# A two-layer attention trunk on one core: first loads moved to other tiles, two weight units queued earlier, copies and side stages placed anew

## The chip, the cores and the metric

The kernel runs on one core of one Trainium2 chip. The metric is the device time of one execution in microseconds, the median of the runs shown. TensorE is called PE below, VectorE DVE, ScalarE ACT, GpSimd POOL, SyncE SP.

## The reference, cut to what matters

256 frames of width 1024 pass two layers. Layer 0 is differential attention, layer 1 a sparse attention in which an indexer chooses 64 keys for each query; each is followed by a squared-ReLU MLP of width 4096. All is float32.

```python
h = rms_norm(x, norm_mix[i])
# layer 0
q, k, v = split(h @ w_in)                      # 1024 columns each
q, k = rope(rms_norm(q, q_g)) * d**-0.5, rope(rms_norm(k, k_g))
p = softmax(where(mask, q @ k.T, -inf))        # 16 maps, two for each of 8 heads
o = rms_norm((p[0] - lam * p[1]) @ v, subln_g) @ w_out
# layer 1
c_q, k, v, k_idx, w_idx = split(h @ w_in)
q, q_idx = c_q @ w_uq, c_q @ w_uq_idx
score = sum_h w_idx[h] * relu(q_idx[h] @ k_idx.T)
idx = top_k(where(mask, score, -inf), 64)
o = softmax(q @ k[idx].T) @ v[idx] @ w_out     # 16 heads
# after each
x = x + o
x = x + relu(rms_norm(x, norm_mlp[i]) @ w1)**2 @ w2
```

## The kernel before

**Products in three parts.** Every float32 operand of a large product is split in two: `hi` is the operand rounded to a reduced form that the matmul takes, `lo` the rest. `mm3` issues three matmuls, hi by hi, hi by lo, lo by hi. So a block of weights (a "unit" of 128 by 2048, 1 MB) is loaded into a `raw` tile, then ACT (or DVE) writes `hi` and DVE writes `lo`, and only then can PE use it. `unit` does that: it issues the load on SP's queue, then the copies, in `pieces` of columns. There are three `raw` tiles and four pairs of hi and lo tiles, so a load waits until the `lo` of the unit three before it has been written.

**Layer 0.** Four projections (j = 0 to 3), each 48 matmuls of 512 columns, give queries and keys of two heads each. For each, `qk_post` (ACT squares, DVE sums, rsqrt, scaling, rope) and `diff_probs` (transposes, scores, exponentials, the difference, transposes to keys) follow. Then two projections of the values (`v_part`), the weighted sums and their normalisation (`diff_out`), and the output projection. The normalisation of the rows of x (`row_scale`, two ACT squares over x) is not needed by the projection: it scales the results later, through `s2c` and `scon`.

**The start.** The first projection's x (transposed) and weights come as one packed input, `first_in`: for k = 0 to 3 a block of 256 columns of x and 512 of weights, then the four further blocks of x. Four loads bring it, in order: block 0 with the small constants, block 1, both into `vt` tiles; blocks 2 and 3 together into the first `raw` tile; the further x into the second. Then the first unit (`ua`, in two loads) into the third `raw` tile. `pack` (constants, the identity for transposes, the gains) is loaded next, then a unit called `ahead`, then x, twice 512 KB; the partner of `ahead` is made after the first projection's matmuls.

**Order.** The program is written in one order, and a scheduler gives each engine its queue from it by priority and by the times that it expects; on the chip each engine then works its queue strictly in order. `spawn` starts a generator as a side stage: it runs until it yields a number of ticks, and goes on after so many matmuls of `mm3`. A yield of 0 or less lets it go on at once. `PAUSE` holds the ticks by the stage's name, 0 where there is none. `HOME` holds choices: `pieces n` of the n-th such unit (default 2); `hi n` which piece DVE copies in place of ACT (default none); `qn`, `qkT`, `aT`, `craw`, `qi`, `vt` 1 for DVE and 0 for ACT; `on` 1 for four ACT copies, 0 for one DVE product; `copied` 1 if keys are copied out of PSUM before they are scaled, 0 if the scaling itself reads PSUM (default 1 for a0 and k1); `ez` from which half of the rows on DVE scales the exponentials (0: both, 2: none).

**Layer 1.** A compressed projection, the indexer (`index`: scores, then eight rounds of max and match-replace for each half of the rows, on DVE), keys (k0, k1), queries (q0, q1), values, `dsa_probs` for each half of the heads, the weighted sums (`dsa_out`), the output projection. `need` runs a side stage to its end.

Of the kernel before, what the change touches and what calls it, by code (L numbers as in the profile page):

```python
# [9 lines left out]
F32 = mybir.dt.float32  # L10
# [6 lines left out]
D = 1024  # L17
# [8 lines left out]
C_NORM = 0  # L26
# [11 lines left out]
S_GAIN, S_INV, S_POS, S_K, S_X, S_END = 0, 8, 16, 32, 32 + 4 * 768, 32 + 4 * 768 + 4 * 256  # L38
# [3 lines left out]

PAUSE = {"a1 transposes 0": 6, "a1 transposes 1": 13, "a1 scores 1": 26, "a2 transposes 0": 6,
# [4 lines left out]

HOME = {"copied a1": 1, "qn a1 0": 1, "qkT a1 0": 1, "hi 1": 1, "pieces 2": 1, "aT a2 1": 1, "aT a1 1": 1,
# [5 lines left out]


@with_exitstack
def trunk(ctx: ExitStack, tc: tile.TileContext, x_in, first_in, pack_in, wf, out):
    nc = tc.nc
    E = ctx.enter_context
    const = E(tc.tile_pool(name="const", bufs=1))
    wraw = E(tc.tile_pool(name="wraw", bufs=3))
    wsp = E(tc.tile_pool(name="wsp", bufs=4))
    act = E(tc.tile_pool(name="act", bufs=4))
    qkp = E(tc.tile_pool(name="qkp", bufs=4))  # L70
    vp = E(tc.tile_pool(name="vp", bufs=2))
# [6 lines left out]
    def acc():  # L78
        return psum.tile([128, 512], F32, name="acc", bufs=4)

    def wk():
        return psum.tile([128, 512], F32, name="wk", bufs=4)
# [5 lines left out]
    nc.scalar.preload_act_table_set("trig_and_small")  # L88


    first = [vp.tile([128, D], F32, name="vt") for _ in range(2)]
    raws = [wraw.tile([128, 2048], F32, name="raw") for _ in range(2)]
    src = []

    def load_first(dst, c, a, b):
        nc.sync.dma_start(dst[:, c:c + b - a], first_in[:, a:b])
        src.append((dst, c, a, b))

    def start(a, n):
        for dst, c, lo, hi in src:  # L100
            if lo <= a and a + n <= hi:
                return dst[:, c + a - lo:c + a - lo + n]

    load_first(first[0], 0, 0, S_K + 768)
    load_first(first[1], 0, S_K + 768, S_K + 2 * 768)
    load_first(raws[0], 0, S_K + 2 * 768, S_X)
    load_first(raws[1], 0, S_X, S_END)

    ident = pack[:, C_ID:C_ID + 128]
    cmask = const.tile([128, 384], F32, name="cmask")  # L110
# [12 lines left out]
    def pause(stage):  # L123
        return PAUSE.get(stage, 0)

    def opt(name, d=0):
        return HOME.get(name, d)

# [11 lines left out]
    def advance(e, to_end=False):  # L140
        was, inside[0] = inside[0], True
        while e in side and (to_end or e[0] <= 0):
            try:
                e[0] = next(e[1])
            except StopIteration:
                side.remove(e)
        inside[0] = was

    def spawn(gen):
        e = [0, gen]  # L150
        side.append(e)
        advance(e)
        return e

    def need(*es):
        for e in es:
            advance(e, True)
# [9 lines left out]
    split = []  # L167
# [3 lines left out]
    def unit(cols=2048, dmas=1, pieces=1, each=None, att=False, homes=None):  # L171


        raw = wraw.tile([128, 2048], F32, name="raw")
        if homes is None:
            hi = wsp.tile([128, 2048], F32R, name="whi")
            lo = wsp.tile([128, 2048], F32R, name="wlo")
        src = bass.AP(tensor=wf.tensor, offset=wf.offset + off[0], ap=[[cols, 128], [1, cols]])
        off[0] += 128 * cols
        step = cols // dmas  # L180
        for i in range(dmas):
            c = slice(i * step, (i + 1) * step)
            nc.sync.dma_start(raw[:, c], src[:, c])
        if att:
            units[0] += 1
            pieces = opt(f"pieces {units[0]}", 2)
        if homes is not None:
            return halves(raw, homes)
        step = cols // pieces
        for i in range(pieces):  # L190
            c = slice(i * step, (i + 1) * step)
            with tc.issue_after(each(i)) if each is not None else ExitStack():
                split[:] = [copy(att and opt(f"hi {units[0]}") == i + 1, hi[:, c], raw[:, c]).ins]
            nc.vector.tensor_tensor(lo[:, c], raw[:, c], hi[:, c].bitcast(F32), op=OP.subtract)  # L194
        return hi[:, :cols], lo[:, :cols]

    def halves(raw, homes):

        res = []
        for c, n, tiles in homes:  # L200
            c = slice(c, c + n)
            hi, lo = [a[:, :n] for a in tiles()]
            nc.scalar.activation(hi, raw[:, c], AF.Copy)
            nc.vector.tensor_tensor(lo, raw[:, c], hi.bitcast(F32), op=OP.subtract)
            res.append((hi, lo))
        return res
# [83 lines left out]
    behind = []  # L290
    ready = []
# [227 lines left out]
    def out_proj(o, us, h, gc, needs=((),) * 4):  # L519


        ps = [[acc() for _ in range(2)] for _ in range(2)]
        for u, (wh, wl) in enumerate(us):
            need(*needs[u])
            wh = wh.rearrange("p (k n) -> p k n", n=D)
            wl = wl.rearrange("p (k n) -> p k n", n=D)
            for n in range(2):
                for t in range(2):
                    c = slice(n * 512, n * 512 + 512)
                    for i in range(2):  # L530
                        k = u * 2 + i
                        ah, al = lhs(o, k, t)
                        mm3(ps[t][n], ah, al, wh[:, i, c], wl[:, i, c], k == 0, k == 7)
                    if u == 3:
                        for j in range(2):
                            c = slice(n * 512 + j * 256, n * 512 + j * 256 + 256)
                            nc.vector.tensor_tensor(x[t][:, c], ps[t][n][:, j * 256:j * 256 + 256], x[t][:, c],
                                                    op=OP.add)
                            make_h(h, gc, t, n, (j,))
# [74 lines left out]
    h = new_h()  # L614
# [13 lines left out]
    for k in range(4):  # L628
        first_h(k)
        v, c = start(S_K + 768 * k + 256, 512), slice(512 * k, 512 * k + 512)  # L630
# [6 lines left out]
        return behind[0]  # L637

    ua.append(unit(dmas=2, pieces=4, each=later_h))
    nc.sync.dma_start(pack, pack_in)  # L640
    ahead = unit(pieces=2)
    for t in range(2):
        nc.sync.dma_start(x[t], x_in[t * 128:(t + 1) * 128, :])
    srow, s2 = row_scale(1)
# [35 lines left out]
    o = new_h()  # L680
# [61 lines left out]
    def take():  # L742
        return ready.pop(0) if ready else pair()

    pr = [[] for _ in range(4)]
    probs, outs = [], []
    for j in range(4):
        ps = [acc() for _ in range(2)]
        project(ps, h, quad(take() if j else ua), 512, by_k=j == 0)
        if j == 0:  # L750
            ready.append([ahead, unit(pieces=2)])
            rope_sines(*angles)
            lam()
        probs.append(spawn(diff_probs(ps, pr[j], f"a{j}")))
# [5 lines left out]
    h = new_h()  # L760
# [16 lines left out]
    h = h1  # L777
# [8 lines left out]
    cqh, cql, _ = parts()  # L786
# [96 lines left out]
    craw = compress()  # L883
# [14 lines left out]
    for n in range(2):  # L898
        ps = [acc() for _ in range(2)]
        c = slice(n * 512, n * 512 + 512)  # L900
# [6 lines left out]
    o = new_h()  # L907
# [19 lines left out]
                    out.append(to_keys(e, f"{half} {hd + r}"))  # L927

    def dsa_out(g, aTs):
        ops = wk()  # L930
        for p in range(2):
            c = p * 256
            for r in range(2):
                rows = slice(64 * r, 64 * r + 64)
                a = aTs[2 * p + r]
                vc = (4 * g + 2 * p + r) * 64
                mm(ops[rows, c:c + 256], vts[1][0][:, vc:vc + 64], a[:, 0:256], start=True, stop=False)
                mm(ops[rows, c + 128:c + 256], vts[1][1][:, vc:vc + 64], a[:, 256:384], start=False, stop=True)
        k = 2 * g
        oh = o[k // 4][0][:, k % 4:k % 4 + 2].rearrange("p a b -> p (a b)")  # L940
        ol = o[k // 4][1][:, k % 4:k % 4 + 2].rearrange("p a b -> p (a b)")
        nc.scalar.activation(oh, ops, AF.Copy)
        nc.vector.tensor_tensor(ol, ops, oh.bitcast(F32), op=OP.subtract)  # L943

    for half in range(2):
        aTs = []
        probs = spawn(dsa_probs(half, aTs))
        v_part(half, h, srow)
        need(probs)
        for i in range(2):  # L950
            dsa_out(2 * half + i, aTs[4 * i:4 * i + 4])
    h = new_h()
    out_proj(o, take() + take(), h, C_NORM + 24)

    def store(t, n, j):
        if (t, n) != (1, 1) and j == 0:
# [124 lines left out]
```

## Time and profile before

| | us |
|---|---|
| median of 3 runs (596.99 to 597.17) | 597.13 |
| the profiled execution | 597.93 |
| its span, first to last instruction | 595.7 |
| PE busy, DVE busy, ACT busy (of the span) | 585.3, 433.3, 348.0 |

Some 2.2 us of the profiled execution lie outside of the span. PE is busy 98% of it. A matmul of 512 columns is shown with 0.39 us, but the next one starts 0.23 us later, so up to 0.16 us of a wait is not shown as idle.

### The profile page before, as it was taken

What the parts mean: (1) busy time and instruction counts of PE and PEld (TensorE: products, weight loads), DVE (VectorE), ACT (ScalarE), POOL (GpSimd) and SP (SyncE); (2) the same over time, 40 slices, a digit from 0 to 9 for tenths busy, and PEclk for the clock granted to TensorE, in tenths of its full rate; (3) what the DMA queues carried; (4) which work ended last, traced back from release to release, by engine and by line L of the source; (5) the groups of instructions that cost most, each with busy time, mean ns of one, the idle gap of its engine ahead of it and who ended that gap; (6) DMA issues with size and microseconds to landing.
All of it is one profiled execution on the core that took longest, in us unless ns stands there. A gap on an engine that the chain in (4) does not pass through costs nothing.

```text
span 595.7 us, 8292 instructions
## 1 busy us (share of the span) xinstructions
PE 585.3 (98%) x3052; PEld 487.1 (82%) x3052; DVE 433.3 (73%) x975; ACT 348.0 (58%) x672; POOL 21.5 (4%) x53
## 2 busy tenths in 40 slices
PE   8999999999999999999999999999999999999997
PEld 6777788888888888888887777778888888888885
DVE  5899987688657656686578999777876567567542
ACT  5878876485545545555366678686755445445420
POOL 6700000000000000000000000000000000000000
PEclk9999999999999999999999999999999999999999
DMA  8865334336555455486442225423566556555401
GB/s 293 332 245 208 142 141 142 142 142 234 194 208 197 169 201 210 169 301 223 142 141 72 81 69 206 141 80 134 205 218 212 176 182 209 183 177 205 142 1 71
DMA packets 15448, 103.34 MB, mean 173 GB/s; under 512 B 1712, under 2 KB 1968, under 8 KB 3760
## 3 DMA queue, kind: packets, MB, share of 16 engines
q1 hardware_dynamic: 15408, 102.82, 48.7%
q8 instruction: 24, 0.39, 0.3%
q14 instruction: 16, 0.13, 0.1%
HBM read 101.76 MB, written 1.05 MB: 173 GB/s over the span
## 4 chain that ended last, share of the span: by engine, by line
PE 83%; DVE 12%; DMA 2%; issue 1%; ACT 1%; SPq 0%; DVEq 0%
PE wk L557 18%; PE acc L213 15%; PE acc L211 15%; PE acc L209 15%; PE wk L560 10%; DVE wlo L194 4%; PE wk L478 2%; PE wk L508 1%; PE acc L557 1%; DMA raw<-in_first 1%; DVE qkss L438 1%; DVE s L489 1%; DMA raw<-in_w 1%; DVE score L880 1%; PE wk L300 1%
## 5 line engine op out<-in xcount | busy, mean ns | idle before, releaser
L194 DVE TENSOR_TENSOR wlo<-raw,whi 128x1024 fp32r<-128x1024 f32 (+2 forms) x193 | 220.2, 1172 | 102.0 <-ACT whi L135 101.8
L135 ACT ACTIVATE whi<-raw 128x1024 fp32r<-128x1024 f32 (+2 forms) x190 | 183.1, 1005 | 98.8 <-PE acc L213 47.2
L211 PE MATMUL acc<-wlo,act 128*128 128x512 f32 x488 | 192.0, 393 | 1.5 <-DVE wlo L194 1.4
L209 PE MATMUL acc<-whi,act 128*128 128x512 f32 x488 | 191.4, 394 | 0.9 <-ACT whi L632 0.9
L213 PE MATMUL acc<-whi,act 128*128 128x512 f32 x488 | 191.9, 393 | 0.0
L557 PE MATMUL wk<-act,whi 128*128 128x512 f32 x480 | 120.6, 392 | 0.0
L211 PEld LDWEIGHTS acc<-wlo,act 128*128 128x128 f32 x488 | 91.8, 188 | 21.6 <-DVE wlo L194 2.2
L209 PEld LDWEIGHTS acc<-whi,act 128*128 128x128 f32 x488 | 91.6, 188 | 20.6 <-issue 1.7
L213 PEld LDWEIGHTS acc<-whi,act 128*128 128x128 f32 x488 | 91.8, 188 | 19.4 <-issue 1.3
L557 PEld LDWEIGHTS wk<-act,whi 128*128 128x128 f32 x480 | 86.8, 189 | 15.8
L560 PEld LDWEIGHTS wk<-act,wlo 128*128 128x128 f32 x480 | 66.0, 190 | 5.1
L560 PE MATMUL wk<-act,wlo 128*128 128x256 f32 x480 | 67.6, 282 | 0.0
L568 ACT ACTIVATE act<-on 128x256 fp32r<-128x256 f32 x64 | 26.4, 415 | 49.9 <-DVE on L567 49.9
L501 ACT ACTIVATE s<-s,nb,rs_r 128x128 f32<-128x128 f32 x64 | 34.2, 536 | 8.2 <-DVE nb L498 8.2
L565 ACT ACTIVATE sq<-wk 128x256 f32<-128x256 f32 x60 | 22.4, 374 | 26.1 <-PE wk L560 26.1
L569 DVE TENSOR_TENSOR act<-on,act 128x256 fp32r<-128x256 f32 x64 | 26.9, 423 | 14.0 <-ACT act L568 12.8
L567 DVE SCALAR_TENSOR_TENSOR on<-sq 128x256 f32<-128x256 f32 x64 | 27.0, 424 | 1.6
L566 DVE TENSOR_TENSOR sq<-wk,sq 128x256 f32<-128x256 f32 x60 | 25.2, 420 | 0.1
L609 DVE SCALAR_TENSOR_TENSOR x<-acc,rows,x 128x256 f32<-128x256 f32 x16 | 7.0, 478 | 14.9 <-PE acc L213 14.9
L304 ACT ACTIVATE act<-wk,pack 128x128 fp32r<-128x128 f32 x48 | 13.8, 378 | 6.8 <-PE wk L300 6.8
L306 DVE SCALAR_TENSOR_TENSOR act<-wk,pack,act 128x128 fp32r<-128x128 f32 x48 | 13.5, 345 | 4.1 <-ACT act L304 4.1
L478 PE MATMUL wk<-qkT 64*128 64x128 f32 (+1 forms) x128 | 14.8, 344 | 0.4 <-DVE act L943 0.3
(208 smaller groups left out, 447.2 us busy)
## 6 DMA issues: line engine op xcount, KB each, us to landing
raw<-in_w SPq DMA_DIRECT2D x91, 1024.0 KB, 4.8
raw<-in_w SPq DMA_DIRECT2D x2, 512.0 KB, 8.8
x<-in_x SPq DMA_DIRECT2D x2, 512.0 KB, 6.8
raw<-in_w SPq DMA_DIRECT2D x1, 984.0 KB, 4.7
raw<-in_w SPq DMA_DIRECT2D x1, 840.0 KB, 4.7
raw<-in_first SPq DMA_DIRECT2D x1, 768.0 KB, 6.5
out_dram<-x SPq DMA_DIRECT2D x3, 256.0 KB, 2.0
raw<-in_first SPq DMA_DIRECT2D x1, 512.0 KB, 7.4
```

The costliest lines, as they stand in the source:

```text
L135: return nc.scalar.activation(out, in_, AF.Copy, **({} if scale is None else dict(scale=scale)))
L194: nc.vector.tensor_tensor(lo[:, c], raw[:, c], hi[:, c].bitcast(F32), op=OP.subtract)
L209: mm(ps, ah, wh, start=first, stop=False)
L211: mm(ps, ah, wl, start=False, stop=False)
L213: mm(ps, al, wh, start=False, stop=last)
L478: mm(ps[r][:, TS[t]], q[rows, t * 128:t * 128 + 128], k[rows, 0:128 * t + 128], start=True, stop=True)
L501: nc.scalar.activation(s[:, TS[t]], s[:, TS[t]], AF.Exp, bias=nb[:, r, t:t + 1], scale=nsc[:, t, r:r + 1], accum_out=z[:, r, t:t + 1])
L557: mm(ps.rearrange("p (a b) -> p a b", b=256), wh[:, k, c], h[k // 4][2][:, :, k % 4], start=k == 0, stop=False)
L560: mm(ps[:, 256:], wl[:, k, c], h[k // 4][0][:, k % 4], start=False, stop=k == 7)
L567: nc.vector.scalar_tensor_tensor(q, r, 0.0, r, op0=OP.max, op1=OP.mult)
L568: nc.scalar.activation(uh[:, m], q, AF.Copy)
L569: nc.vector.tensor_tensor(ul[:, m], q, uh[:, m].bitcast(F32), op=OP.subtract)
```

## The change

- The first loads: blocks 2 and 3 come in two loads of 384 KB rather than one of 768 KB, and these and the further x go into three `qkT` tiles. The `raw` tiles are all free for units.
- The two units for j = 1 (before: `ahead` and a partner made after the first projection) are made together behind the first unit, ahead of the load of `pack` and of x. So SP's queue has them before `pack` and x. `behind` is set to the last `hi` copy of these units, and the row squares of x are ordered behind it on ACT.
- `dsa_out` becomes a side stage that the output projection needs; it yields `pause("sums g")` first.
- `PAUSE` and `HOME` get new values.

```diff
-         "a2 transposes 0": 6, "a2 scores 0": 14, "a1 keys 0": 22, "a1 keys 1": 38,
-         "out2": 31, "out3": 30, "q0 transposes 0": 41, "q1 transposes 0": 7, "probs 01": 16
+         "a2 transposes 0": 8, "a2 scores 0": 13, "a1 keys 0": 23, "a1 keys 1": 36,
+         "out2": 28, "out3": 24, "q0 transposes 0": 29, "q1 transposes 0": 2, "probs 01": 20
...
- HOME: "copied a1": 1, "qn a1 0": 1, "ez 1 2": 2
+ HOME: "qn a0 0": 1, "qn a0 1": 1, "copied a3": 1, "pieces 3": 1, "pieces 6": 1,
+       "on 0": 1, "on 2": 1, "hi 14": 1, "hi 15": 2, "qi 0": 1
...
-    first = [vp.tile([128, D], F32, name="vt") for _ in range(2)]
-    raws = [wraw.tile([128, 2048], F32, name="raw") for _ in range(2)]
-    load_first(first[0], 0, 0, S_K + 768)
-    load_first(first[1], 0, S_K + 768, S_K + 2 * 768)
-    load_first(raws[0], 0, S_K + 2 * 768, S_X)
-    load_first(raws[1], 0, S_X, S_END)
+    load_first(vp, "vt", 0, S_K + 768)
+    load_first(vp, "vt", S_K + 768, S_K + 2 * 768)
+    load_first(qkp, "qkT", S_K + 2 * 768, S_K + 3 * 768)
+    load_first(qkp, "qkT", S_K + 3 * 768, S_X)
+    load_first(qkp, "qkT", S_X, S_END)
...
     ua.append(unit(dmas=2, pieces=4, each=later_h))
+    ready.append([unit(pieces=2), unit(pieces=2)])
+    behind[:] = split
     nc.sync.dma_start(pack, pack_in)
-    ahead = unit(pieces=2)
...
         if j == 0:
-            ready.append([ahead, unit(pieces=2)])
             rope_sines(*angles)
...
     def dsa_out(g, aTs):
+        yield pause(f"sums {g}")
         ops = wk()
...
-            dsa_out(2 * half + i, aTs[4 * i:4 * i + 4])
+            sums.append(spawn(dsa_out(2 * half + i, aTs[4 * i:4 * i + 4])))
     h = new_h()
-    out_proj(o, take() + take(), h, C_NORM + 24)
+    out_proj(o, take() + take(), h, C_NORM + 24, [[e] for e in sums])
```

The tables are shown by what differs; all other entries stay.

## Rows read from the trace of the kernel before

**Rows 1.** PE's waits over the span: us in total, times, longest.
```profile
PE acc L211 <- DVE wlo L194: 1.4, 2, 0.9
PE wk L463 <- DVE qn L423: 1.2, 3, 0.7
PE wk L508 <- DVE s L700: 1.0, 2, 0.5
PE acc L209 <- ACT whi L632: 0.9, 1, 0.9
PE wk L478 <- DVE act L943: 0.3, 1, 0.3
```

**Rows 2.** Timeline of PE: start, duration, line, what, idle before.
```profile
18.97 0.50 PE L211 MATMUL acc<-wlo,act 128*128 128x512 f32 x1 [0.49 <-DVE wlo L194]
...
44.29 0.39 PE L213 MATMUL acc<-whi,act 128*128 128x512 f32 x1
44.51 0.39 PE L209 MATMUL acc<-whi,act 128*128 128x512 f32 x1
...
353.15 0.41 PE L463 MATMUL wk<-pack,qn 128*128 128x128 f32 x2
```

**Rows 3.** The chain that ended last, 0 to 130 us: start, us, what.
```profile
1.64 6.54 DMA raw<-in_first
...
10.99 5.58 DMA raw<-in_w
...
61.14 1.09 PE wk L463 x8
```

**Rows 4.** Stretches: length, busy of each engine (instructions), clock, DMA share, GB/s.
```profile
15.00:30.00 15.00, 13.62 (x59) 10.60 (x58) 12.41 (x35) 12.74 (x22) 10.95 (x21) 1.00 0.84 333
30.00:45.00 15.00, 14.96 (x79) 11.79 (x79) 15.00 (x42) 11.82 (x23) 0.66 (x2) 1.00 0.68 238
...
75.00:90.00 15.00, 15.00 (x90) 12.52 (x89) 13.39 (x42) 10.97 (x31) 0.00 (x0) 1.00 0.39 140
...
330.00:345.00 15.00, 14.34 (x69) 11.68 (x68) 15.00 (x55) 10.30 (x19) 0.00 (x0) 1.00 0.41 141
```

**Rows 5.** The page's DMA issues: count, size, median us from issue to landing.
```profile
x<-in_x SPq DMA_DIRECT2D x2, 512.0 KB, 6.8
...
pack<-in_pack SPq DMA_DIRECT2D x1, 256.0 KB, 9.2
```

**Rows 6.** Timeline of SP's queue, 0 to 15 us.
```profile
3.76 0.45 SPq L640 DMA_DIRECT2D pack<-in_pack  x1
...
11.36 0.91 SPq L643 DMA_DIRECT2D x<-in_x  x2
```

**Rows 7.** Timeline of ACT at 11 us.
```profile
11.07 0.63 ACT L135 ACTIVATE whi<-raw 128x512 fp32r<-128x512 f32 x1 [0.52 <-DMA raw<-in_w]
```

**Rows 8.** Timeline of DVE, 17 to 47 us.
```profile
17.69 2.38 DVE L194 TENSOR_TENSOR wlo<-raw,whi 128x1024 fp32r<-128x1024 f32 x2 [1.85 <-ACT whi L135]
...
21.20 0.17 DVE L273 TENSOR_SCALAR rowv<-rowss 128x2 f32<-128x2 f32 x1 [0.35 <-ACT qn L271]
...
31.00 0.68 DVE L133 COPY qn<-acc 128x512 f32<-128x512 f32 x1
31.60 0.74 DVE L448 TENSOR_TENSOR qn<-qn,rs_r 128x256 f32<-128x256 f32 x2
...
46.24 0.42 DVE L448 TENSOR_TENSOR qn<-qn,rs_r 128x256 f32<-128x256 f32 x1
```

**Rows 9.** Timeline of DVE, 288 to 353 us.
```profile
288.56 2.29 DVE L194 TENSOR_TENSOR wlo<-raw,whi 128x2048 fp32r<-128x2048 f32 x1 [3.93 <-ACT whi L135]
...
308.74 0.17 DVE L273 TENSOR_SCALAR rowv<-rowss 128x2 f32<-128x2 f32 x1 [2.75 <-ACT qn L271]
...
314.44 0.75 DVE L134 TENSOR_SCALAR qn<-wk,rs_r 128x512 f32<-128x512 f32 x1
...
352.71 0.30 DVE L423 TENSOR_TENSOR qn<-rp,rp 128x128 f32<-128x128 f32 x1
```

More of the change, by code (lines that the diff above doesn't have):

```diff
@@ L41 @@
             0.0014142135623842478, 0.00027424818836152554, 5.3182957344688475e-05, 1.0313385246263351e-05]
-PAUSE = {"a1 transposes 0": 6, "a1 transposes 1": 13, "a1 scores 1": 26, "a2 transposes 0": 6,
[4 rows of a table removed]
-HOME = {"copied a1": 1, "qn a1 0": 1, "qkT a1 0": 1, "hi 1": 1, "pieces 2": 1, "aT a2 1": 1, "aT a1 1": 1,
[5 rows of a table removed]
+PAUSE = {"a1 transposes 0": 6, "a1 transposes 1": 13, "a1 scores 1": 26, "a2 transposes 0": 8,
[4 rows of a table added]
+HOME = {"qn a0 0": 1, "qn a0 1": 1, "qkT a1 0": 1, "hi 1": 1, "pieces 2": 1, "pieces 3": 1, "aT a2 1": 1,
[6 rows of a table added]
 @with_exitstack
@@ L88, in trunk, with load_first @@
     nc.scalar.preload_act_table_set("trig_and_small")
-    first = [vp.tile([128, D], F32, name="vt") for _ in range(2)]
-    raws = [wraw.tile([128, 2048], F32, name="raw") for _ in range(2)]
     src = []
-    def load_first(dst, c, a, b):
-        nc.sync.dma_start(dst[:, c:c + b - a], first_in[:, a:b])
-        src.append((dst, c, a, b))
+    def load_first(pool, name, a, b):
+        dst = pool.tile([128, 1024], F32, name=name)
+        nc.sync.dma_start(dst[:, :b - a], first_in[:, a:b])
+        src.append((dst, a, b))
     def start(a, n):
-        for dst, c, lo, hi in src:
+        for dst, lo, hi in src:
             if lo <= a and a + n <= hi:
-                return dst[:, c + a - lo:c + a - lo + n]
-    load_first(first[0], 0, 0, S_K + 768)
-    load_first(first[1], 0, S_K + 768, S_K + 2 * 768)
-    load_first(raws[0], 0, S_K + 2 * 768, S_X)
-    load_first(raws[1], 0, S_X, S_END)
+                return dst[:, a - lo:a - lo + n]
+    load_first(vp, "vt", 0, S_K + 768)
[3 more added lines that the diff above has]
+    load_first(qkp, "qkT", S_X, S_END)
     ident = pack[:, C_ID:C_ID + 128]
@@ L943, in dsa_out @@
         nc.vector.tensor_tensor(ol, ops, oh.bitcast(F32), op=OP.subtract)
+    sums = []
     for half in range(2):
```

19 rows, old and new, of tables (HOME, PAUSE) are left out of this document.

## The prediction

> **What bounds the kernel now.** I read PE's waits first, because PE is busy nearly all of the time and only what it waits for can be won. [rows 1] holds nine waits after the start that the view shows as idle, 4.8 us together. Matmuls start 0.22 to 0.23 us apart while each is shown with 0.39 [rows 2], so each such wait hides another 0.16: 4.8 + 9 x 0.16 = 6.2 us. That is the most that any rearrangement gives. The reader should see who ends them: seven end with DVE's data, one (0.9) with ACT's first copies, and one (0.3) with a DVE instruction that frees PSUM.
>
> Then the chain of waits [rows 3]. It starts with the load of blocks 2 and 3, which lands at 1.64 + 6.54 = 8.18; goes on with a unit's load (`ahead`) issued at 10.99, when its `raw` tile is free, and landing at 16.57; and from there runs almost only over ACT and DVE until PE takes over at 61.14 and, after one more wait for DVE, for good. The stretches say the same: DVE is busy 15.00 of 15 from 30 to 45 and again from 330 to 345, while 75 to 90 leaves it 1.6 idle with PE at 15.00 [rows 4]. So there are two places where something else holds PE back, the first 72 us and about 326 to 380 us. Elsewhere the kernel is PE's own work, which the change leaves as it is.
>
> Of the 6.2, the three waits for L463 count 1.2; one of the three falls at 61 us [rows 3], so I give the second place two thirds, 0.8, and the 0.3 for PSUM: with 3 x 0.16 it has 1.6, the first place 4.6.
>
> **The first loads.** Blocks 2 and 3 in two parts let block 2 land earlier. Half of the 768 KB should be there some 1.5 us before the whole, at an estimated 6.7, and PE's wait of 0.9 + 0.16 before block 2 mostly goes. But what is late next is the first unit: ACT waited for it until 11.07, with nothing else to do for 0.52 [rows 7], and the bytes ahead of it are the same. Its first `lo` follows a `hi` copy of 0.63 and a subtraction of much the same length, so it is there at some 12.4 in both kernels. PE, now a microsecond early, waits for it. I take 0.2 us of 1.1 for PE at the end of the first projection; the ends are 0 and 1.1.
>
> The Trainium skill says in Perfetto Trace Analysis, DMA Optimizations, that splitting DMAs may let some work start sooner if the DMA engines are generally idle. They are not idle here (share 0.84 from 15 to 30 us, [rows 4]); by that sentence too the split gives the 0.2 rather than the 1.1.
>
> **The two units ahead of `pack` and x.** Nothing holds their `raw` tiles any longer, so SP issues them right behind the first unit. `pack`, issued behind that unit at 3.76 [rows 6], landed 9.2 later, at 12.96 [rows 5]; the first unit is down shortly before, at some 12.3. At the 333 GB/s of [rows 4] a megabyte takes 3.1 us, so `ahead` lands at 15.4 in place of 16.57 and its partner at 18.5. DVE's first `lo` of `ahead` started at 17.69 after 1.85 idle [rows 8], 1.1 after the landing; now it starts at about 16.5: 1.2 us earlier. PE needs the partner 24 matmuls after the first of them, at 18.97 - 0.65 + 5.5 = 23.8 [rows 2], and by then it is split. So PE's two waits for `wlo` (1.4 + 2 x 0.16 = 1.7) go, and PE enters the third projection about 2 us earlier.
>
> The price: `pack` lands at 19.3, x at 20.9 and 22.4 in place of 11.36 + 6.8 = 18.2 [rows 5, 6] (the median of both halves). `pack` has cover: its first user that counts is the transposes of a0 after 35 us. The squares of x on ACT end about 1.1 after x, at 23.5, and the row scale on DVE, which began at 21.20 after 0.35 idle [rows 8], begins there. What covers these 2.3 us is the partner's `lo`, the sums of the first projection and its copies, all ready before. I take 0.3 gained, the idle time; the ends are -2.3 (DVE stands still for x) and +1.0 (its short dependent steps are filled with long ones).
>
> **DVE's own load, 16 to 72 us.** `qn a0` on DVE adds two copies of 512 columns out of PSUM; one takes DVE 0.60 until the next instruction starts (31.00 to 31.60, [rows 8]): 1.2 more. Of it I count 0.7, since DVE waits for loads and for x around 20 us anyway; ends 0 and 1.2. `copied a1` and `qn a1 0` dropped take away the very copy at 31.00: 0.6 less; the scaling then reads PSUM, at about the same length. `copied a3` widens a DVE copy from 256 to 512 columns, at most half of 0.60: 0.3 more. `pieces 3` joins two subtractions, under 0.1, not counted.
>
> Sum of the first place: 1.2 + 0.3 - 0.7 + 0.6 - 0.3 = 1.1 earlier for DVE, and the 0.2 of PE's own: **1.3 us**. The ends: -2.0 (x stops DVE, 2.3, and the rest is +0.6 - 0.3), and +3.9, if of the 4.6 only the wait for the first unit (about 0.7) is left.
>
> The Trainium skill, Perfetto Trace Analysis, Optimizing Scalar/DVE Operations, says that if DVE is saturated, offloading some work to Scalar may make sense; `qn a0` does the reverse. [rows 4] has DVE saturated from 30 us on but 2.6 of 15 us idle from 15 to 30, where these two copies stand. By the sentence the whole 1.2 would count, and the first place would give 0.8.
>
> **The second place.** `hi 14` and `hi 15` move 2048 and 1024 columns from ACT to DVE. Before 288.56 DVE had waited 3.93, before 308.74 2.75 [rows 9]: they cost nothing there. `qi 0` puts one more scaling of 0.75 [rows 9] into DVE's queue ahead of the indexer's rope; PE has key matmuls to do meanwhile, so I take 0; without them it costs 0.7. `on 0`, `on 2`, `pieces 6`, `out2` and `out3` lie where PE does not wait (75 to 90 in [rows 4] and later), `ez 1 2` behind PE's last wait: nothing. The side stage for `dsa_out` does nothing at all: `PAUSE` has no "sums", so it yields 0, and `spawn` runs it through on the spot, in the order it had.
>
> What remains is that q0's transposes may come 12 matmuls earlier, 12 x 0.23 = 2.7 us of PE's time, and q1's 5. q0's stand at 353.15 [rows 2], right behind the rope that ends at 352.71 + 0.30 = 353.01 [rows 9], so they move only if DVE's rope does. The 1.6 of PE's waits here is what can be won. I take 0.5; the ends are +1.6 and -1.5: PE comes to them at 350.45 rather than 353.15, has the eight transposes of k1 to do first (1.1, as in [rows 3]), and stands until 353.01.
>
> **Sum.** 1.3 + 0.5 = 1.8. The profiled execution of 597.93 becomes 596.1; it lay 0.8 above the median of 597.13, so the median becomes **595.3 us**, 0.3% less.
>
> **Rivals.**
>
> *Given back.* PE's lead of 2 us meets a DVE that is hardly ahead, and its waits for L508 and L463 [rows 1] grow by what those at the start lost. For it: the chain runs over DVE to 61 us [rows 3], and DVE is full from 30 to 45 [rows 4]. One form of it: without its copy, a1's accumulators are free only after the scaling that ends at 46.24 + 0.42 [rows 8], while the fourth projection, which writes them next, was at work at 44.51 [rows 2]; if DVE keeps its order, PE stands there for up to 2 us. Against it: DVE has slack after 75 us, so side stages can slide back and PE spend its lead on matmuls. Gain -0.5 to 1.2: 596 to 597.6, no change to be told.
>
> *Slower: x stops DVE.* If the row scale stands ahead of the partner's `lo` in DVE's queue, everything behind it starts 2.3 late, and only 0.6 - 0.3 of it comes back: 2.0 lost, 599.1. It decides once x lands later than DVE's other work lasts. For it: DVE stood 0.35 for these squares already [rows 8]. Against it: two copies and a unit more are ready before x now.
>
> *Slower: wrong order in the second place.* q0's transposes move up in PE's queue, the rope does not: 1.5 lost there, 0.3 won in the first place: 598.3.
>
> *Both places whole.* 3.9 and 1.6 won: 591.6.
>
> **The numbers.** Forecast (gain 1.2 to 3.9): 0.50. Both places whole: 0.08. Given back: 0.25. x stops DVE: 0.10. Wrong order: 0.07. About 0.2%, 1.2 us, is what a measurement of this kernel tells from no change. So faster 0.58, the same 0.25, slower 0.17. The forecast's own range is 593.2 to 595.9. The range for all cases, 592.3 to 598.4, leaves out most of the case of both places whole and of that of x.
>
> **What would show it.** Right: PE's waits for `wlo` L194 gone from the list; the one for `whi` L632 gone or short, and one for the first unit before 12.4 us in its place; DVE's first `lo` of 1024 columns at about 16.5 us; the row scale at about 23.5; some wait for L508 or L463 left before 72 us. Wrong: a wait of over 1 us at the fourth projection's start or at q0's transposes; more idle time of DVE before the row scale than 0.35; PE's list empty between 12 and 380 us.

## The result: 601.1 us against 597.1, 0.7% slower

| | before | after |
|---|---|---|
| median, us (6 runs each) | 597.06 (595.75 to 597.25) | 601.12 (598.86 to 601.35) |
| ratio, 95% interval | | 1.0070 (1.0058 to 1.0082) |
| profiled execution, its span | 597.93, 595.7 | 601.23, 598.9 |

The forecast was 595.3 and the range ended at 598.4. The time lies outside of it, on the side that had 0.17. Lines of the changed kernel stand 1 to 3 higher than those of before: the `lo` subtraction is L195, the row squares L272, the sines L399, the table load behind them L403, `mm3` L210, L212 and L214; in the kernels of the experiments some of them move by one or two more. The list of changed table entries above leaves out one: `ez 1 3` goes as well.

PE's waits after (us in total, times, longest), beside [rows 1]:

```profile
PE acc L210 <- DVE whi L134: 1.9, 1, 1.9
PE acc L212 <- DVE wlo L195: 1.2, 1, 1.2
PE wk L464 <- DVE qn L424: 1.2, 3, 0.6
PE wk L509 <- DVE s L702: 0.6, 2, 0.3
PE wk L479 <- DVE act L945: 0.3, 1, 0.3
```

The list looks hardly longer than before. But two of its waits are single and long, and both are for DVE. Where the time went shows best in the start of the matmul of `mm3` that has n others ahead of it, after less before (worked out from the two timelines of PE; a minus is earlier, a lead). The profiled execution of before lies about 1 us above the medians of its runs (597.93 against 596.7 to 597.1), so of a lead here about 1 us is no gain by the runs.

```
n        24     48     72     84     96    108    144    288    383   1000   1400
after -1.20  -0.90  -1.69  -2.89  -0.78  +2.97  +3.14  +3.35  +3.43  +3.25  +3.41
```

PE is 2.9 us ahead at n = 84 and 3.0 behind at n = 108. From there on little changes (0.4). So the loss lies between 28 and 37 us. Stretches of the kernel after (columns as in [rows 4]):

```profile
15.00:30.00 15.00, 13.06 (x59) 10.50 (x57) 9.36 (x28) 9.91 (x20) 9.19 (x23) 1.00 0.79 323
30.00:32.00 2.00, 0.80 (x3) 0.26 (x3) 2.00 (x7) 2.00 (x5) 0.00 (x0) 0.60 0.01 4
32.00:37.50 5.50, 5.50 (x14) 4.30 (x15) 5.43 (x14) 3.84 (x4) 0.00 (x0) 0.52 0.52 191
37.50:45.00 7.50, 7.50 (x39) 6.30 (x38) 6.31 (x15) 3.35 (x5) 0.00 (x0) 1.00 0.76 281
```

DVE, which had 12.41 of 15 us to do from 15 to 30 before [rows 4], has 9.36: it stands still. And the granted clock is 0.60 from 30 to 32 us and 0.52 in the 5.5 us after: it was 1.00 up to 30.4, behind PE's first wait, and fell while PE stood in the second. Who holds DVE is on ACT's timeline:

```profile
17.65 2.00 ACT L136 ACTIVATE whi<-raw 128x1024 fp32r<-128x1024 f32 x2
23.83 0.22 ACT L399 ACTIVATE sn<-ang 128x16 f32<-128x16 f32 x1 [4.19 <-POOL ang L389]
...
24.40 1.04 ACT L272 ACTIVATE qn<-x 128x1024 f32<-128x1024 f32 x1
...
25.55 1.28 ACT L403 ACT_TABLE_LOAD   x1
26.85 1.06 ACT L272 ACTIVATE qn<-x 128x1024 f32<-128x1024 f32 x1
```

ACT has finished the partner's `hi` copies at 19.65 and then stands 4.19 us for POOL's angles, because the sines are next in its queue; the row squares are behind the sines, and the table load stands between the two squares. In the kernel before ACT had them the other way round:

```profile
18.51 1.04 ACT L271 ACTIVATE qn<-x 128x1024 f32<-128x1024 f32 x1
...
20.03 1.04 ACT L271 ACTIVATE qn<-x 128x1024 f32<-128x1024 f32 x1
...
22.50 2.02 ACT L135 ACTIVATE whi<-raw 128x1024 fp32r<-128x1024 f32 x2
24.39 0.22 ACT L398 ACTIVATE sn<-ang 128x16 f32<-128x16 f32 x1
```

In both programs the sines have an edge (`issue_after(split[0])`) that holds them behind the partner's `hi` copies. Before, these came after the squares (22.50), so the edge also kept the sines behind the squares. The change brings the copies to 17.65 and holds the squares behind the same copies; then nothing orders the sines and the squares any more. The angles come later too: the last of POOL's operations on them ends at 22.07 before and at 23.80 after.

```profile
21.87 0.20 POOL L388 TENSOR_SCALAR ang<-ang 128x16 f32<-128x16 f32 x1
```
```profile
18.19 0.25 POOL L348 TENSOR_SCALAR tp<-rn 128x16 f32<-128x16 f32 x1
...
19.12 1.34 POOL L348 TENSOR_SCALAR tp<-a 128x16 f32<-128x16 f32 x1
...
23.60 0.20 POOL L389 TENSOR_SCALAR ang<-ang 128x16 f32<-128x16 f32 x1
```

Of the last three lines the second has the same form as the first and takes five times as long. It starts while DVE runs a `lo` subtraction (19.14 to 21.48). After the change both units are split while POOL is at work on the angles, and from 15 us on four of its operations take over 1.0; before it was two. On DVE:

```profile
25.57 1.29 DVE L134 COPY qn<-acc 128x512 f32<-128x512 f32 x2 [3.74 <-ACT qn L272]
28.03 0.17 DVE L274 TENSOR_SCALAR rowv<-rowss 128x2 f32<-128x2 f32 x1 [1.17 <-ACT qn L272]
...
29.19 0.69 DVE L134 CAST whi<-raw 128x1024 fp32r<-128x1024 f32 x1
...
30.70 1.22 DVE L195 TENSOR_TENSOR wlo<-raw,whi 128x1024 fp32r<-128x1024 f32 x1
```

The copies of a0 wait 3.74 for the first square, which writes its squares into the `qn` tile; the row scale waits 1.17 for the second one. Only behind them come the next unit's `hi` copy (29.19) and `lo` (30.70), for which PE waits. The chain that ended last runs the same way (start, us, what):

```profile
20.54 1.03 POOL ang L349
24.19 0.31 ACT cs L401
24.50 1.04 ACT qn L272 x2
25.55 1.28 ACT L403
26.85 1.16 ACT qn L272 x2
29.19 0.69 DVE whi L134
30.04 0.60 DVE qkss L439
30.79 1.14 DVE wlo L195
31.97 0.80 PE acc L212
32.77 0.43 PE acc L214
33.20 0.43 PE acc L210
```

Its last two rows are at the lower level: matmuls 0.43 apart rather than 0.23. The account, from start to start of PE's matmuls: 2.1 lost at 29.94 (shown as 1.9), 1.5 at 31.97 (shown as 1.2), and the twelve matmuls from 31.97 on, up to the start of the next at 37.26, take 5.28 in place of 12 x 0.227: 2.6. Together 6.2, which turns a lead of 2.9 into 3.3 behind.

### The profile page after: what moved, and what is told of

It reads as the page before. It is cut to its first block, busy times and chain, and to the rows that moved or that the text cites. A ratio compares the mean times of both kernels' runs of the same rounds, so it can differ in the third digit from the quotient of the medians.

```text
span 598.9 us, 8292 instructions
## 1 busy us (share of the span) xinstructions
PE 588.4 (98%) x3052; PEld 489.8 (82%) x3052; DVE 434.8 (73%) x981; ACT 344.1 (57%) x668; POOL 19.4 (3%) x53
## 4 chain that ended last, share of the span: by engine, by line
PE 85%; DVE 9%; POOL 3%; issue 1%; ACT 1%; DMA 1%; DVEq 0%
PE wk L558 18%; PE acc L212 16%; PE acc L214 16%; PE acc L210 15%; PE wk L561 10%; DVE wlo L195 2%; PE wk L479 2%; PE wk L509 2%; PE acc L558 1%; DVE s L490 1%; POOL tp L348 1%; DVE qkss L439 1%; PE wk L464 1%; DVE score L881 1%; PE wk L301 1%
## 5 line engine op out<-in xcount | busy, mean ns | idle before, releaser
L195 DVE TENSOR_TENSOR wlo<-raw,whi 128x1024 fp32r<-128x1024 f32 (+2 forms) x191 | 220.0, 1182 | 97.2 <-ACT whi L136 96.8
L136 ACT ACTIVATE whi<-raw 128x1024 fp32r<-128x1024 f32 (+2 forms) x186 | 180.2, 1009 | 94.0 <-PE acc L214 46.8
L212 PE MATMUL acc<-wlo,act 128*128 128x512 f32 x488 | 193.5, 397 | 1.2 <-DVE wlo L195 1.2
L210 PE MATMUL acc<-whi,act 128*128 128x512 f32 x488 | 192.7, 397 | 1.9 <-DVE whi L134 1.9
L214 PE MATMUL acc<-whi,act 128*128 128x512 f32 x488 | 193.2, 396 | 0.0
L212 PEld LDWEIGHTS acc<-wlo,act 128*128 128x128 f32 x488 | 92.7, 190 | 21.6 <-DVE wlo L195 2.2
L210 PEld LDWEIGHTS acc<-whi,act 128*128 128x128 f32 x488 | 92.3, 190 | 21.2 <-DVE whi L134 2.4
L214 PEld LDWEIGHTS acc<-whi,act 128*128 128x128 f32 x488 | 92.6, 190 | 19.7 <-issue 1.2
L566 ACT ACTIVATE sq<-wk 128x256 f32<-128x256 f32 x60 | 22.4, 373 | 26.4 <-PE wk L561 26.4
```

The lines of the kernel that those rows point to most:

```text
L136: return nc.scalar.activation(out, in_, AF.Copy, **({} if scale is None else dict(scale=scale)))
L210: mm(ps, ah, wh, start=first, stop=False)
L212: mm(ps, ah, wl, start=False, stop=False)
L214: mm(ps, al, wh, start=False, stop=last)
```

## The experiments

Theory A: the sines (and with them POOL's angles) stand ahead of the row squares on ACT, and DVE stands behind the squares. Rivals: x itself lands too late (B), the copies of a0 on DVE (C), a loss from the tables or the loads whatever the order of ACT (D). Some expectations name two more, T (the new tables cost the rest) and X (a late x costs something in any order). The runs were made in four groups, with the kernel before beside each: medians of 597.07 (first to fourth), 596.73 (fifth to eighth), 596.92 (ninth to eleventh) and 596.82 (twelfth). So a few tenths between runs of two groups tell nothing by themselves.

**First: the sines held behind the squares.** In `row_scale` the last square is kept in a list `squared`, and:

```diff
 def rope_sines(ang, b):
-        with tc.issue_after(split[0]):
+        with tc.issue_after(squared[0]):
```

> The changed kernel with one edge more: the sines of the rope tables are queued on ACT behind the row squares, not ahead of them. Theory A (ACT's queue: the squares stand behind sines that wait for POOL's angles, and DVE's copy for the third projection stands behind the row scale): the squares run at 19.7 to 21.8, DVE's row scale starts at about 22 instead of 28.03, PE's waits of 1.9 and 1.2 at 30 to 32 us shrink to under 1 together, TensorE's clock stays at the high level, and the time falls by 4 to 6 us to 595 to 597. Theory B (x itself lands too late behind the two units, 19.0 and 20.3): the row scale cannot start much before 27, the time stays at 600 to 601. Theory C (DVE has too much work with a0's two copies): DVE full from 22 us, the waits stay over 2 us, 599 to 601.

Measured: 598.32 (597.89 to 598.45), 2.8 below the kernel after, where theory A had 4 to 6; to before 1.0015 (1.0002 to 1.0028). ACT and then DVE in its profile:

```profile
17.84 2.00 ACT L136 ACTIVATE whi<-raw 128x1024 fp32r<-128x1024 f32 x2
19.74 1.05 ACT L272 ACTIVATE qn<-x 128x1024 f32<-128x1024 f32 x1
...
20.78 1.05 ACT L272 ACTIVATE qn<-x 128x1024 f32<-128x1024 f32 x1
...
24.26 0.22 ACT L400 ACTIVATE sn<-ang 128x16 f32<-128x16 f32 x1 [2.34 <-POOL ang L390]
```
```profile
22.16 1.28 DVE L134 COPY qn<-acc 128x512 f32<-128x512 f32 x2
23.36 0.15 DVE L274 TENSOR_SCALAR rowv<-rowss 128x2 f32<-128x2 f32 x1
...
26.55 0.69 DVE L134 CAST whi<-raw 128x1024 fp32r<-128x1024 f32 x1
...
28.29 1.22 DVE L195 TENSOR_TENSOR wlo<-raw,whi 128x1024 fp32r<-128x1024 f32 x1
```

The squares follow the `hi` copies without a gap, so x was there in time: B falls. (The edge also takes the table load out from between the squares; what it alone cost there, 1.4, and the sines' share are not told apart.) The waits of 1.9 and 1.2 and the clock's fall are gone, one wait of 0.9 at 29.56 is left. PE's last `mm3` matmul starts at 590.46 in place of 594.55 on the two chains, 4.1 earlier. The time gains only 2.8, since the last store, issued 1.2 after that matmul, takes 2.9 us to land in this profile and 1.8 in those of before and after.

**Second: a0's copies back on ACT**, the sines left where they are.

```diff
-HOME = {"qn a0 0": 1, "qn a0 1": 1, "qkT a1 0": 1, ...
+HOME = {"qkT a1 0": 1, ...
```

> The changed kernel with a0's two copies out of PSUM back on ACT. Theory A: the squares end at 28.0 as before, the row scale and DVE's copy for the third projection behind it, so the waits stay and the time stays at 600 to 601.5. Theory C: DVE has 1.2 us less in its queue and no longer stands 3.74 before these copies; the time falls by 2.5 to 4 us.

Measured: 602.59 (602.31 to 602.66). PE's waits:

```profile
PE acc L210 <- DVE rs_a L233: 1.6, 1, 1.6
PE acc L212 <- DVE wlo L195: 1.2, 1, 1.2
```

Both stand as in the kernel after, at 30.2 and 32.2, and the clock falls again. By themselves the copies are not the cause: C falls as the whole answer. The time is 1.5 above the kernel after, and 1.1 above what theory A allowed; why was not followed.

**Third and fourth: each half of the change alone.** Third: the new loads, units and side stage with the old `PAUSE` and `HOME`. Fourth: the kernel before with the new `PAUSE` and `HOME`.

> The new loads and the new place of the two units, with the old tables of pauses and choices. Theory A: the same order on ACT, sines ahead of squares, so the same loss before 45 us; 600 to 602. Theory D (the new tables cost the time, not the loads): 594 to 596.5.

> The kernel before with the new tables alone, loads and units as before. Theory A: the squares stand ahead of the sines in ACT's queue, the row scale starts at about 21 to 22; within 1.5 us of the kernel before, 596 to 598.5. Theory D: 600 to 602.

Measured: 602.40 (601.67 to 603.02) and 602.75 (602.67 to 604.39). The longest waits of the third, then of the fourth:

```profile
PE acc L211 <- DVE wlo L194: 1.9, 1, 1.9
PE acc L209 <- DVE rs_a L232: 1.6, 1, 1.6
```
```profile
PE wk L733 <- ACT on L724: 3.0, 1, 3.0
```

The third has the loss at 30 us without any new table entry, as A wants, and 0.4 more than A allowed: its sines run at 23.99, its squares at 24.56 and 27.00. The fourth missed what I expected: it is 1.2 ahead of before at n = 144, then PE reaches layer 0's output transposes before `on` is there, waits 3.0 at 94 us, and the clock falls again. So with the old loads these tables lose time at another place, and PE ends 4.5 behind the profile of before. The kernel after doesn't have that wait.

**Fifth: the third with the first one's edit** (old tables, sines behind the squares).

> The new loads and the side stage with the tables of the kernel before (the third experiment, 602.4), and the sines held behind the row squares. Order theory (A: the lateness comes from the sines that stand ahead of the row squares on ACT): the squares start by 21.5 us, DVE's row scale by 24, no wait of PE over 1.3 us between 28 and 35 us, no clock below 1.0 there; 3 to 5 us faster than the third experiment, 597.4 to 599.4. If the 1.1 us that the first experiment lay above the kernel before come from the new tables (theory T), this lands at 597.1 or below. If a later x costs something of its own whatever the order (theory X), it stays at 598.0 or above, and so does every kernel with the new loads.

Measured: 596.86 (596.66 to 597.06), 5.5 below the third, and 1.0000 (0.9989 to 1.0012) to before. One edge in ACT's order takes back all that the loads had cost. That is A again, and against D: the loads cost nothing when the order is right. With the old tables they gain nothing either that the runs can tell. It is also as fast as theory T asked for; the sixth tells why that isn't T.

**Sixth and seventh: layer 0's output stage as before**, on the first experiment (sixth) and on the fourth (seventh).

```diff
-"out2": 28, "out3": 24        "on 0": 1, "on 2": 1
+"out2": 31, "out3": 30
```

> The kernel after with the sines held behind the row squares, and with layer 0's output stage as before: on 0 and on 2 on DVE, out2 and out3 with pauses of 31 and 30. Theory T (the new entries for the output stage cost the rest): PE's wait of 0.5 at 86 us for ACT's on is gone, PE's last matmul comes 0.5 to 1 us earlier than in the first experiment, 597.2 to 597.8. Theory X (late x): no change against the first experiment, 598.0 to 598.5. If DVE lacks the room for the two on copies, a wait of PE for qn or s grows by about as much as the 0.5, and the time stays too.

> The kernel before with all new tables but the four entries of layer 0's output stage (on 0, on 2, out2, out3). If these entries made the fourth experiment's wait of 3.0 at 94 us (theory T), that wait and the clock's fall behind it are gone: 4.5 us faster than it, 598.2, or lower, as its start was 1.2 us ahead of the kernel before at 36 us: 596 to 598.2. If the wait comes from the order of the other stages, it stays at 602 to 603.

Measured: 597.15 (596.33 to 597.74) and 603.01 (602.46 to 603.57). The seventh's wait only changes its name:

```profile
PE wk L733 <- DVE on L726: 3.6, 1, 3.6
```

So these four entries don't make the fourth's wait; which of the other entries does was not followed further. The sixth is 1.2 faster than the first (0.8 with the difference of before beside them taken off), as theory T had it, but not for T's reason: the 0.5 for `on` is still there (now for DVE), and its last `mm3` matmul starts only 0.1 earlier. Its last store takes 1.8 rather than 2.9; in the two profiles that is the difference.

**Eighth, tenth and eleventh: a0's copies again, with the order mended.** Eighth: the sixth with the second's edit. Tenth: the first with the second's edit. Eleventh: the eighth without `"copied a3": 1`.

> The sixth experiment with the two copies of a0's accumulators back on ACT. The prediction counted 0.7 us for these copies on DVE (ends 0 and 1.2). If that price is right, DVE's row scale or the first subtraction behind it comes 0.7 to 1.2 earlier and the time is 0.3 to 0.7 below the sixth experiment's. If ACT's queue is what limits the start now that DVE only waits for the row squares, the copies delay the squares or the next hi copies by up to 1.2 and the time is the same or up to 1 us above it.

> The first experiment (the kernel after, sines behind the row squares, 598.3) with the two copies of a0's accumulators on ACT; the output stage's entries are those of the kernel after. The eighth experiment gained 1.0 on the sixth by this. If the copies' price of 1.0 holds by itself, 597.3 or below, and if the output stage's entries are what separates the first from the sixth, 597.3 and not 596.2. If the first experiment's late last store (2.9 us) was a chance of that program, 596.2.

> The eighth experiment (596.2) with a3's first copy narrow again, which the prediction priced at 0.3 of DVE's time in the first place. If DVE is what PE waits for there, up to 0.3 faster: 595.8 to 596.2; if the wide copy frees the accumulators earlier than it costs, the same or up to 0.5 slower.

Measured: 596.16 (596.03 to 596.57); 595.90 (595.57 to 596.15), to before 0.9986 (0.9977 to 0.9995); 596.49 (596.18 to 597.08). The eighth gained more than the 0.3 to 0.7 expected (1.0). The tenth came out nearest to the 596.2 expected if the late last store was a matter of the first experiment's program; its own takes 1.8. The tenth has the lowest median of all kernels here and differs from the kernel after by two small edits; they are worth 5.2 us (5.0 by the two ratios to before). DVE in its profile, beside that of the first:

```profile
22.34 0.17 DVE L274 TENSOR_SCALAR rowv<-rowss 128x2 f32<-128x2 f32 x1 [0.25 <-ACT qn L272]
...
24.78 0.68 DVE L134 CAST whi<-raw 128x1024 fp32r<-128x1024 f32 x1
...
26.56 1.21 DVE L195 TENSOR_TENSOR wlo<-raw,whi 128x1024 fp32r<-128x1024 f32 x1
```

Without the 1.29 of the two copies the row scale begins 1.0 earlier and the `lo` 1.7 earlier, and no wait of PE is left between 12.4 and 48 us: PE is busy in 15.00 of 15 from 15 to 30 and from 30 to 45. The eleventh is 0.3 above the eighth, 0.1 with the difference of before taken off, so the runs alone don't tell it from no change. In its profile PE ends 0.5 later than in the eighth's, with a wait of 0.6 at 57.9 us for DVE's scaling, which reads the accumulators itself. So the wide copy of a3, which I priced at a loss of 0.3, is no loss, and probably a small gain.

**Ninth: pack and x loaded ahead of the two units again**, everything else as after.

```diff
-    ready.append([unit(pieces=2), unit(pieces=2)])
     behind[:] = split
     nc.sync.dma_start(pack, pack_in)
...
+    ready.append([unit(pieces=2), unit(pieces=2)])
```

> The kernel after with pack and x loaded ahead of the two units again (they still have free raw tiles and follow x at once), nothing else changed and the sines not held back. Order theory: x is down early, so the program itself has the row squares ahead of the sines on ACT; the row scale ends by 24 us, no wait of PE over 1.3 us between 28 and 35 us and no clock below 1.0 there. The units come later instead, so PE enters the third projection 1 to 2 us behind the first experiment. 2 to 4 us below the kernel after: 597 to 599. If the late x was not what put the sines first or if the lateness on DVE comes from the tables, it stays at 600 or above. The fourth experiment's wait at 94 us may come back with these tables on other loads; then 3.5 us more and that wait in the list.

Measured: 605.50 (605.07 to 606.80). The order came out as A says: with x early the squares run at 13.86 and 15.08, the row scale at 16.27, the sines behind them at 21.96, and there is no wait from 28 to 35 us. More than the place of x differs, though: `behind` is set ahead of the units here, so the squares stand behind the first unit's `hi` copies alone. This run alone doesn't tell whether the late x or this edge had put the sines first. The kernel after, built without `behind[:] = split` (not run), has the sines first all the same; so the edge is not what decides, but that x is loaded behind the units. But the units are late instead, far more than the 1 to 2 us that I expected, and the fourth's wait is back:

```profile
PE wk L734 <- ACT on L725: 3.0, 1, 3.0
PE acc L210 <- ACT whi L136: 1.9, 2, 1.6
PE acc L212 <- DVE wlo L195: 1.5, 1, 1.5
```

The last two lines' waits lie at 18.9 and 21.1 us for the most part, with matmuls 0.43 apart behind them. At n = 72 PE is 5.3 behind the first experiment. This is not the order of before either: there `ahead` was queued ahead of x, here both units are behind it.

**Twelfth: the second place.** The tenth with the second layer's entries as before (q0 41, q1 7, probs 01 16; `hi 14`, `hi 15`, `qi 0` out; `ez 1 2` and `ez 1 3` back).

> The tenth experiment (595.9) with everything that the change did to the second layer's part of the tables undone: q0's and q1's transposes at 41 and 7 matmuls, probs 01 at 16, hi 14, hi 15 and qi 0 on ACT, ez 1 2 and ez 1 3 placed as before. The prediction gave this place 0.5 (ends +1.6 and -1.5). If that holds, this is 0.5 slower, 596.4, and PE's waits between 326 and 385 us grow by as much. If the place gives nothing, as the matching positions of PE in the two profiles suggest, it stays within 0.3 of 595.9 and PE's last matmul within 0.3 of the tenth experiment's. If the entries cost something, it is faster.

Measured: 596.24 (595.63 to 596.56), 0.34 above the tenth, in another group; to before 0.9983 (0.9971 to 0.9994), against the tenth's 0.9986. So the runs don't tell the two apart. From n = 383 to n = 1400 PE loses 0.28 on the tenth, with one new wait of 0.4 at 313 us for the indexer's keys. By the profiles the place is worth at most some 0.3, and not by q0's transposes: PE's waits at 334 and 348 us are the same 0.8 and 0.55 in both.

The lead over the profile of before in six of these kernels, worked out as above:

```
n           24     48     84     96    108    144    288    383   1400
first    -1.14  -0.74  -2.70  -2.70  -1.48  -1.69  -0.60  -0.58  -0.68
fifth    -0.91  -0.53  -2.52  -2.52  -2.52  -2.01  -1.11  -1.12  -1.15
eighth   -0.70  -0.26  -2.24  -2.24  -2.22  -2.49  -1.78  -1.74  -1.77
tenth    -0.76  -0.31  -2.30  -2.30  -2.20  -2.48  -2.11  -2.11  -2.19
eleventh -0.66  -0.25  -2.23  -2.23  -2.14  -2.42  -1.24  -1.23  -1.27
twelfth  -0.47  -0.06  -2.05  -2.05  -1.75  -2.02  -1.64  -1.61  -1.41
```

## Why the prediction was wrong, point by point

**The failed step is the price of the late x.** "The squares of x on ACT end about 1.1 after x, at 23.5, and the row scale [...] begins there." In the kernel after it began at 28.03. I costed when x lands and left out what stands ahead of the squares in ACT's queue. x was even earlier than the 20.9 and 22.4 that I had estimated: in the first experiment both squares run from 19.74 on without waiting. But the change makes x late, puts the squares behind the partner's `hi` copies, and brings these copies forward, behind which the sines had been held. The order that came of it has the sines first, and they wait for POOL's angles, which end at 23.80. The angles themselves came 1.7 later than before, most of it (two times some 0.8) in the two more of POOL's operations that now fall within a `lo` subtraction; the prediction has no term for that. The step's ends were -2.3 and +1.0 for DVE; DVE stood still for 3.74 + 1.17 = 4.9. In [rows 8] it was 0.35, and more than that was one of the signs of being wrong. What DVE's stand cost PE was two waits, 3.6, and 2.6 at the lower clock, for which the sum had no term either.

The Trainium skill, Perfetto Trace Analysis, says under Tensor Engine Instruction that ACT, DVE and GpSimd work strictly first in, first out. The trace agrees: the same squares start at 24.40 behind the sines and at 19.74 ahead of them.

**The nearest rival was "x stops DVE"** (599.1, chance 0.10). Place and victim are right: DVE stands before the row scale and everything behind it is late. Its condition, x later than DVE's other work, was not what decided, and it left out the clock. One of the six executions of the kernel after came with a mean clock of 1.0: it took 598.86, with a span of 596.6, 2.3 below the profiled one, close to the 2.6 worked out above and to the rival's time. Two more, with a mean clock of 0.997, took 600.53 and 601.00. That the fall of the clock is what separates the 598.86 is read from these executions, not shown by an experiment.

**The first loads.** The share of 0.84 that I quoted is of 15 to 30 us, where these loads don't lie; from 2 to 8 us, where they do, it was 0.93, so the reading stands. I took 0.2 of 1.1 and expected PE to wait for the first unit. PE's lead at the end of the first projection is 0.9 after, 0.1 to 0.7 in the other kernels of the table, which have the same loads. Right within its ends, small.

**The units ahead of x.** DVE's first `lo` of 1024 columns was to start at 16.5; it starts at 15.66. PE was to enter the third projection 2 us earlier; it is 2.9 ahead at n = 84, 2.3 in the tenth. Right for the start. But the fifth, with the same loads, the order mended and the old tables, is no faster than before: there the lead alone is worth nothing at the end.

**a0's copies on DVE**: 0.7, ends 0 and 1.2. By PE's last matmul they cost 1.5 (first against tenth) and 1.0 (sixth against eighth). I had them run in DVE's idle time around 20 us. They can't: in the first experiment they start at 22.16, behind the squares that use the `qn` tile, right ahead of the row scale. The whole 1.2, which the prediction drew from the sentence of the Trainium skill (Perfetto Trace Analysis, Optimizing Scalar/DVE Operations), would have been nearer.

**Copied a3, the output stage, the side stage.** a3's wide copy is no loss, where I had one of 0.3. `on` and the pauses of out2 and out3 change nothing in the first and sixth but the last store. The side stage for `dsa_out` does nothing, as predicted: built with a plain call in its place, the program has the same instructions in the same order on every engine.

**Given back** (0.25). It depends on the tables. Of the 2.30 that the tenth leads by at n = 96, 2.19 are left at n = 1400. But the fifth, with the old tables, leads by 2.52 up to n = 108 and by 1.15 at the end, and the runs have it level with before: there what the rival describes came true. In the first experiment 2.0 of 2.7 are given back, 1.2 of them at the wait for `lo` at 29.56, where the copies of a0 hold DVE, and 1.1 between n = 144 and n = 288.

So the two terms that cost most were the late x and a0's copies. With both undone PE gains 2.2 on the profile of before; by the runs the tenth is 1.0 faster than before (596.92 beside it), where I forecast 1.8 for a kernel with a0's copies on DVE. That the other terms come to about this is no proof of each: the fifth shows that the loads alone give nothing.

## What to carry to other kernels

When a load is moved back, don't stop at when it lands: list what each engine has ahead of its first user once that user is late, and what those instructions wait for. An engine that waits in order hands on the latest of all of them, here POOL's angles to ACT, ACT's squares to DVE and DVE's subtraction to PE. And try loads and placements together, and look at the order that comes of them: old loads with new tables and new loads with old tables both lost over 5 us here, the first to a wait at 94 us that the kernel after does not have, the second to ACT's order, which one edge mended.

## What the runs showed of the hardware

- In the kernel after PE waited 2.1 us up to 29.94 and 1.5 up to 31.97. The granted clock was 1.00 up to 30.4 and 0.50 from 30.4 to 37.2, the lower of the two levels (1.2 of 2.4 GHz); matmuls of 512 columns were 0.43 apart rather than 0.23. This cost 2.6 beside the 3.6 of the waits. One wait of 3.7 up to 94.3 us in the seventh was followed by 0.50 from 95.9 to 99.3; behind one of 1.1 up to 29.56 in the first the clock stayed at 1.00.
- POOL's operations on 128 by 16 elements slow down beside DVE: in all 14 profiles, from 15.6 us to the end of the angles, each one that starts within a `lo` subtraction of 1024 columns takes 1.0 to 1.3 us, and each other one at most 0.32. Why was not tested.
- The table load between the squares took 1.28, and the next square started 0.02 after it. The two squares lie 2.45 apart, and 1.04 without it, so it cost 1.4. The Trainium skill, ScalarE: Activation LUTs, What ACT_TABLE_LOAD costs, gives 2.66 for a switch with the drain; the drain of that sum is not seen here.
- The last store (128 KB) took 2.9 us in the first experiment's profile and 1.8 in the 13 others, before and after among them. The other ten executions of that kernel (597.89 to 598.45) fit the profiled one (598.23), so it is probably no chance of one execution. Its cause stays open.
